# A hybrid pooling and state-space layer on one core: the scan's groups of four heads taken in pairs, nine small transposes in one place, and the first gate sum next to a pair

## The chip, the core and the metric

One core of a Trainium2 chip runs the whole layer in one launch. The metric is device time in microseconds (us), the median of three runs. Five engines work side by side, each through its own queue in order: PE (TensorE, the matmuls; PEld is its weight loading), DVE (VectorE), ACT (ScalarE), POOL (GpSimd) and SP (SyncE, which issues most transfers).

## What is computed

256 prompt positions and 32 sample positions are held as 288 columns (features lie on partitions). All matrices and data are fp32. The part that the change touches is the mixer of the layer, cut to what matters:

```python
proj = rmsnorm(x) @ w_in             # columns u | z | xBC | dt
xbc  = silu(causal_dwconv(xBC))      # xs (2048), B (2 groups x 128), C (2 x 128)
dt   = softplus(dt_raw + bias); a = dt * A        # 32 heads
acum = cumsum(a) ; lmat = exp(acum_l - acum_s) for s <= l
cb   = C_l . B_s                     # one per group of 16 heads
y    = (cb * lmat) @ (xs * dt) + exp(acum) * (C @ h_prev) + D * xs
y    = y * silu(z)
y    = y * rsqrt(mean(y*y) + eps) * norm_g        # per group of 16 heads
mix  = concat[pool, y] @ w_out
```

After it come the residual, the FFN (`w_up`, a short convolution, `silu(gate) * value`, `w_down`) and its norm, which the change leaves alone.

## The kernel before

**The large projections.** Every weight matrix is read from HBM in `raw` tiles of 1 MB. Each is split, 1024 columns at a time, into a high part and a low part: ACT copies `whi` (L129), then DVE subtracts to get `wlo` (L130). With an activation that was split in the same way, a product is three matmuls of 128x288 (`mm3`, L135 to L137: hi by hi, hi by lo, lo by hi). One pair of `whi` and `wlo`, called a weight tile below, feeds 24 such matmuls, and there are four buffers of each part, so the split can run at most four tiles ahead of PE. A call of `project` for 256 columns is a block of 96 matmuls, four weight tiles, into two accumulators `acc` (a PSUM pool of five, `acc_ps`).

**The order of the blocks.** First a block of 768 columns (B, C, the first 256 of xs), then seven blocks for the rest of xs, then eight for z, then four for u. In Python the scan's steps are written between the blocks; the scheduler of the language places every instruction on its engine's queue by its own timeline.

**The decays.** `g` (running sums of dt times A) and `dt` are 32 rows. Nine PE transposes (three each of `g`, `dt` and `dec`, L413 to L415) bring them to positions on partitions, three tiles `ptok` in PSUM; DVE copies them to `tok` and `tokd` (L416, L417). Then `pcb` (L430 to L432) makes the products of C and B, masked to `cbt`.

**A group of four heads (`ssd_four`, L442 to L485).** There are eight. SP fetches `gb` (the rows of g for four heads, broadcast to all partitions), `h0t` and `xw` (xs with positions on partitions, which went through DRAM as `xs_d` by way of `blocks_out`, one buffer `blocks`). ACT makes `ce`, then 12 activations write `m` from `gb` and `tok` (L464), then one Exp over all of `m` (L467). DVE scales `xw` (L459) and multiplies `m` by `cbt` (L469). PE then makes 16 products, which are 32 passes in the trace, into two PSUM tiles `py` (L476 to L482). DVE adds them into xs (L485). `gb`, `h0t`, `xw`, `ce` and `m` have two buffers each; `py` lies in the small PSUM pool `aux` with three buffers.

**When a group runs.** `XS_RATE` and `Z_RATE` say how many groups are written behind each block of xs and z. The gate multiplies the finished xs by silu(z) (`gate_in`, `gate_silu`, `gate_mul`), sums squares on POOL (`gsum`), and `gate_rstd` takes the mean by a matmul `psum_g` (L489) in `aux`, then Sqrt on ACT (L236) and a reciprocal on DVE (L237).

Of the kernel before, what the change touches and what calls it, by code (L numbers as in the profile page):

```python
# [8 lines left out]
F32 = mybir.dt.float32  # L9
F32R = mybir.dt.float32r  # L10
AF = mybir.ActivationFunctionType
ALU = mybir.AluOpType
# [4 lines left out]
P = 128  # L17
# [4 lines left out]
NT = NP_ + NS  # L22
# [3 lines left out]
HEADS = 32  # L26
# [3 lines left out]
NX = D_SSD // P  # L30
# [5 lines left out]
HALF = NF // 2  # L36
MW = 416
EVAC = 100
XS_RATE = (0, 0, 0, 1, 0, 1, 0, 1)
Z_RATE = (1, 0, 1, 0, 1, 1, 1, 0)  # L40


@with_exitstack
def body(
# [25 lines left out]
    act, dve, pool, pe, sp = nc.scalar, nc.vector, nc.gpsimd, nc.tensor, nc.sync  # L70
# [7 lines left out]
    acc_ps = ctx.enter_context(tc.tile_pool(name="acc_ps", bufs=5, space=PSUM))  # L78
# [3 lines left out]
    def aux(shape, name):  # L82
        return aux_ps.tile(shape, F32, tag="aux", name=name)
# [97 lines left out]
    mean = const.tile([P, P], F32, name="mean")  # L181
# [35 lines left out]
    start = ExitStack()  # L217
# [35 lines left out]
    for kb, n in chunks:  # L253
# [12 lines left out]
        for k in range(kb, kb + n):  # L266
# [19 lines left out]
            for m in range(6):  # L286
                c = slice(m * P, (m + 1) * P)
# [5 lines left out]
    p_ = aux([P, NT], "pdt")  # L293
# [23 lines left out]
    id32 = ident[:HEADS, :HEADS]  # L317
# [63 lines left out]
    dt = htile("dt", tag="gsum")  # L381
# [7 lines left out]
    g = mp.tile([HEADS, 2, MW], F32, tag="m", bufs=2, name="g")[:, 0, :]  # L389
# [11 lines left out]
    dec = htile("dec", tag="gsum")  # L401
# [4 lines left out]
    tok = mp.tile([P, 3, 2, HEADS], F32, name="tok")  # L406
    tokd = const.tile([P, 3, HEADS], F32, name="tokd")
    dec_s = mp.tile([HEADS, 4, NS], F32, name="dec_s")
    dve.tensor_copy(dec_s, dec[:, NP_:].unsqueeze(1).broadcast_to([HEADS, 4, NS]))
    dec_s = dec_s.rearrange("h r s -> h (r s)")  # L410
    for b, (go, o) in enumerate(((0, 0), (256, P), (288, NT - P))):
        p_ = aux([P, 3, HEADS], "ptok")
        pe.transpose(p_[:, 0, :], g[:, go : go + P], id32)  # L413
        pe.transpose(p_[:, 1, :], dt[:, o : o + P], id32)
        pe.transpose(p_[:, 2, :], dec_s if b == 2 else dec[:, o : o + P], id32)  # L415
        dve.tensor_copy(tok[:, b, :, :], p_[:, 0:2, :])  # L416
        dve.tensor_copy(tokd[:, b, :], p_[:, 2, :])  # L417

    bc = []
    for i in range(4):  # L420
        o = btile("bc")
# [17 lines left out]
    xs = []  # L439
    elast = const.tile([P, HEADS + 32], F32, name="elast")  # L440

    def ssd_four(q):  # L442

        c = slice(2 * P * q, 2 * P * q + 2 * P)
        gb = mp.tile([P, 4, MW], F32, tag="gb", bufs=2, name="gb")
        sp.dma_start(out=gb, in_=g_d[4 * q : 4 * q + 4, :].unsqueeze(0).broadcast_to([P, 4, MW]))
        h0t = mp.tile([P, 2 * P], F32, tag="h0t", bufs=2, name="h0t")
        sp.dma_start(out=h0t, in_=state_ssd[:, c])
        xw = mp.tile([P, 3, 2 * P], F32, tag="xw", bufs=2, name="xw")
        sp.dma_start(out=xw[:, 0:2, :], in_=xs_d[:NP_, c].rearrange("(b p) c -> p b c", p=P))  # L450
        sp.dma_start(out=xw[:, 2, :], in_=xs_d[NT - P :, c])
        ce = mp.tile([P, 4, NS], F32, tag="ce", bufs=2, name="ce")
        act.activation(ce, gb[:, :, 384:], AF.Exp)
        act.activation(elast[:, 4 * q : 4 * q + 4], gb[:, :, MW - 1], AF.Exp)
        cs = bc[2 + q // 4][:, NP_:]
        dve.tensor_tensor(ce, ce, cs.unsqueeze(1).broadcast_to([P, 4, NS]), op=ALU.mult)
        w = tok[:, :, 1, 4 * q : 4 * q + 4].unsqueeze(3).broadcast_to([P, 3, 4, 64])
        x4 = xw.rearrange("p b (r q) -> p b r q", r=4)
        dve.tensor_tensor(x4, x4, w, op=ALU.mult)  # L459
        m = mp.tile([P, 4, MW], F32, tag="m", bufs=2, name="m")  # L460
        for j in range(4):
            h = 4 * q + j
            for b, (lo_, hi_) in enumerate(((0, 256), (256, 384), (384, MW))):
                act.activation(  # L464
                    m[:, j, lo_:hi_], gb[:, j, lo_:hi_], AF.Relu, bias=tok[:, b, 0, h : h + 1], scale=-1.0
                )
        act.activation(m, m, AF.Exp, scale=-1.0)  # L467
        gi = q // 4
        dve.tensor_tensor(m, m, cbt[:, gi : gi + 1, :].broadcast_to([P, 4, MW]), op=ALU.mult)  # L469
        ys = [aux([P, NT], "py") for _ in range(2)]  # L470
        for k in range(4):
            for j in range(4):
                c = slice(64 * j, 64 * j + 64)
                y = ys[j // 2][64 * (j % 2) : 64 * (j % 2) + 64, :]
                if k == 0:
                    pe.matmul(y[:, 0:256], xw[:, 0, c], m[:, j, 0:256], start=True, stop=False)  # L476
                elif k == 1:
                    pe.matmul(y[:, 128:256], xw[:, 1, c], m[:, j, 256:384], start=False, stop=True)  # L478
                elif k == 2:
                    pe.matmul(y[:, 256:], xw[:, 2, c], m[:, j, 384:], start=True, stop=False)  # L480
                else:
                    pe.matmul(y[:, 256:], h0t[:, c], ce[:, j, :], start=False, stop=True)  # L482
# [4 lines left out]
    def gate_rstd(t):  # L487
        p_ = aux([P, NT], "psum_g")
        pe.matmul(p_, mean, gsum[t], start=True, stop=True)  # L489
# [13 lines left out]
    gsum = [mp.tile([P, NT], F32, tag="gsum", bufs=2, name="gsum") for _ in range(2)]  # L503
# [31 lines left out]
    fours = list(range(NX // 2))  # L535
    gates = list(range(NX))
    done = [-1]
    rg = []

    def run_fours(n):  # L540
        for _ in range(n):
            if fours and 2 * fours[0] + 1 < len(xs):
                q = fours.pop(0)
                ssd_four(q)
                done[0] = 2 * q + 1

    def run_gates():
        while gates and gates[0] in zs and gates[0] <= done[0]:
# [7 lines left out]
    for i in range(NX // 2):  # L556
        ps = project(win, [(O_Z + 256 * i, 256)], xn, K16)
        for j in range(2):
            gate_in(2 * i + j, ps[j])
        if i == 0:  # L560
            xs_conv(NX // 2 - 1)
        run_fours(Z_RATE[i])
        for j in range(2):
            gate_silu(2 * i + j)
        run_gates()
        if i == 4:
            assert gates[0] >= 8
            rg.append(gate_rstd(0))
        if i > 4:
            for t in range(3 * i - 15, min(8, 3 * i - 12)):  # L570
                dve.tensor_tensor(xs[t], xs[t], rg[0], op=ALU.mult)
    run_fours(NX)
    run_gates()
    assert not gates and not fours

# [76 lines left out]
    for t in range(NX):  # L652
# [4 lines left out]
        _, low = split_from(a, xs[t], g_ssd[:, t : t + 1])  # L657
# [150 lines left out]
    for grp in ((0, 1), (2,), (3,), (4,), (5,), (6,), (7,)):  # L808
# [5 lines left out]
        if grp[0] == 2:  # L814
            j = grp[0] // 2 - 1
# [51 lines left out]
    for k in range(KD):  # L867
# [15 lines left out]
        else:  # L883
            q = out_temp()
# [357 lines left out]
```

## Time and profile before

| | |
|---|---|
| time, median of 3 runs | 1320.09 us (1319.91 to 1320.91) |
| the profiled execution's own time | 1319.88 us |
| its span (first to last instruction) | 1317.90 us |
| granted TensorE clock | 0.999 |
| DVE busy | 894.7 us (68%) |
| ACT busy | 670.9 us (51%) |
| POOL busy | 232.6 us (18%) |
| HBM | 188 GB/s over the span |

An engine's share says how busy it was over all stages. Rows of the timeline give the start in us, the length in us, engine, line, operation, output and inputs, and how many like instructions follow each other (x8); in brackets stands idle time ahead of it and what ended it. A matmul's length is its latency; the next one starts long before it ends, so what a matmul costs is read from start to start. Rows of groups give the sum of busy time, the mean length of one in ns, and the idle time ahead of them.

### The profile page before, as it was taken

To read this page: it belongs to the slowest core of one execution; us is meant where nothing else is said; L and a number is where in the kernel's file an instruction comes from. 1 tells how busy PE (TensorE), PEld (TensorE's weight loads), DVE (VectorE), ACT (ScalarE), POOL (GpSimd) and SP (SyncE) were. 2 spreads that over 40 slices of the span, in tenths; PEclk is the share of its full clock that TensorE was granted. 3 is DMA by queue.
4 is the path that set the end of the run, shared out by engine and by line. 5 is a ranking of instruction groups with operands and counts; after the bars stand their busy time and mean duration, and the time that the engine had idled before them with its cause. 6 is when DMAs were issued, how large, how long until landed. Compare 5 with 4: busy or idle time off the path is not lost.

```text
span 1317.9 us, 25200 instructions
## 1 busy us (share of the span) xinstructions
PE 1310.9 (99%) x10067; PEld 1298.6 (99%) x10067; DVE 894.7 (68%) x1486; ACT 670.9 (51%) x1010; POOL 232.6 (18%) x368
## 2 busy tenths in 40 slices
PE   9999999999999999999999999999999999999998
PEld 9999999999999999999999999999999999999997
DVE  7999997779654599967766743346666666664544
ACT  7558876446543466644444433334444444444443
POOL 7321221221430200211211200001111111101110
PEclk9999999999999999999999999999999999999999
DMA  8668874465665556666544445455544554466663
GB/s 327 200 206 280 277 233 144 150 227 205 203 211 192 180 169 221 185 185 194 172 165 160 156 172 173 155 177 180 173 161 164 177 172 160 163 235 187 204 178 110
DMA packets 104068, 249.81 MB, mean 190 GB/s; under 512 B 64064, under 2 KB 69504, under 8 KB 81680
## 3 DMA queue, kind: packets, MB, share of 16 engines
q1 hardware_dynamic: 101584, 242.72, 56.0%
q0 software_dynamic: 1936, 5.31, 1.4%
q8 instruction: 78, 1.28, 0.4%
q14 instruction: 38, 0.31, 0.1%
q10 hardware_dynamic: 432, 0.19, 0.1%
HBM read 236.23 MB, written 11.95 MB: 188 GB/s over the span
## 4 chain that ended last, share of the span: by engine, by line
PE 99%; DMA 1%; ACT 0%; SPq 0%; issue 0%; DVE 0%
PE acc L135 31%; PE acc L137 31%; PE acc L136 31%; PE py L476 1%; PE acc_x L135 1%; PE acc_x L137 1%; PE acc_x L136 1%; DMA raw<-in_w_first 1%; PE pst L773 0%; PE run_a L1114 0%; PE low L1112 0%; PE run_b L1127 0%; PE py L478 0%; PE pdt L297 0%; PE py L482 0%; PE py L480 0%
## 5 line engine op out<-in xcount | busy, mean ns | idle before, releaser
L130 DVE TENSOR_TENSOR wlo<-raw,whi 128x1024 fp32r<-128x1024 f32 (+1 forms) x386 | 463.0, 1201 | 313.2 <-ACT whi L129 310.7
L129 ACT ACTIVATE whi<-raw 128x1024 fp32r<-128x1024 f32 (+1 forms) x386 | 400.2, 1038 | 463.3 <-PE acc L136 370.5
L135 PE MATMUL acc<-hn,whi 128*128 128x288 f32 x1360 | 393.3, 294 | 0.0
L136 PE MATMUL acc<-hn,whi 128*128 128x288 f32 x1360 | 392.7, 293 | 0.0
L137 PE MATMUL acc<-hn,wlo 128*128 128x288 f32 x1360 | 391.9, 293 | 0.0
L135 PEld LDWEIGHTS acc<-hn,whi 128*128 128x128 f32 x1360 | 253.3, 188 | 0.4 <-ACT hn L873 0.4
L136 PEld LDWEIGHTS acc<-hn,whi 128*128 128x128 f32 x1360 | 253.3, 188 | 0.1
L137 PEld LDWEIGHTS acc<-hn,wlo 128*128 128x128 f32 x1360 | 253.3, 188 | 0.0
L135 PE MATMUL acc<-xn,whi 128*128 128x288 f32 x688 | 202.5, 296 | 0.7 <-ACT whi L276 0.7
L136 PE MATMUL acc<-xn,whi 128*128 128x288 f32 x688 | 200.3, 293 | 0.0
L137 PE MATMUL acc<-xn,wlo 128*128 128x288 f32 x688 | 195.0, 295 | 0.0
L135 PE MATMUL acc<-fa,whi 128*128 128x288 f32 x660 | 194.0, 294 | 0.0
L136 PE MATMUL acc<-fa,whi 128*128 128x288 f32 x660 | 193.4, 293 | 0.0
L137 PE MATMUL acc<-fa,wlo 128*128 128x288 f32 x660 | 193.1, 293 | 0.0
L135 PEld LDWEIGHTS acc<-xn,whi 128*128 128x128 f32 x688 | 129.3, 188 | 2.6 <-ACT whi L276 1.2
L136 PEld LDWEIGHTS acc<-xn,whi 128*128 128x128 f32 x688 | 129.2, 188 | 0.4
L137 PEld LDWEIGHTS acc<-xn,wlo 128*128 128x128 f32 x688 | 126.5, 188 | 0.0
L135 PEld LDWEIGHTS acc<-fa,whi 128*128 128x128 f32 x660 | 124.1, 188 | 0.0
L137 PEld LDWEIGHTS acc<-fa,wlo 128*128 128x128 f32 x660 | 123.9, 188 | 0.0
L136 PEld LDWEIGHTS acc<-fa,whi 128*128 128x128 f32 x660 | 123.9, 188 | 0.0
L925 POOL COPY fc_stage<-ebuf 128x4 f32<-128x4 f32 x88 | 27.7, 315 | 513.7 <-DVE ebuf L924 513.7
L921 POOL COPY ebuf<-pf 128x2 f32<-128x2 f32 x88 | 75.5, 858 | 129.5 <-DVE fc L931 83.0
(312 smaller groups left out, 1742.2 us busy)
## 6 DMA issues: line engine op xcount, KB each, us to landing
raw<-in_w_up SPq DMA_DIRECT2D x80, 1024.0 KB, 4.8
raw<-in_w_in SPq DMA_DIRECT2D x38, 1024.0 KB, 5.0
raw<-in_w_down SPq DMA_DIRECT2D x32, 1024.0 KB, 4.8
raw<-in_w_out SPq DMA_DIRECT2D x23, 1024.0 KB, 4.8
raw<-in_w_down SPq DMA_DIRECT2D x16, 768.0 KB, 4.3
raw<-in_w_up SPq DMA_DIRECT2D x8, 896.0 KB, 4.5
gb<-g_d SPq DMA_DIRECT2D x8, 832.0 KB, 6.2
raw<-in_w_first SPq DMA_DIRECT2D x7, 768.0 KB, 10.0
```

The costliest lines, as they stand in the source:

```text
L129: act.activation(hi, raw[:, k : k + n, :], AF.Copy)
L130: dve.tensor_tensor(lo, raw[:, k : k + n, :], hi.bitcast(F32), op=ALU.subtract)
L135: pe.matmul(out, wh, a[:, 0, :], start=start, stop=False)
L136: pe.matmul(out, wh, a[:, 1, :], start=False, stop=False)
L137: pe.matmul(out, wl, a[:, 0, :], start=False, stop=stop)
L476: pe.matmul(y[:, 0:256], xw[:, 0, c], m[:, j, 0:256], start=True, stop=False)
L921: pool.tensor_copy(e[:, 258:260], pf[:, 4:6, i])
L925: pool.tensor_copy(fc_stage[:, :, :, i], e[:, 256:324].rearrange("p (s c) -> p s c", c=34)[:, :, 0:2])
```

## The change

The eight groups of four are taken two by two: behind the last xs block, and behind the third, fifth and seventh z block (counted from one). `ssd_four` is cut in two. `four_in` is everything up to the product of `m` and `cbt`; `four_out` holds the PE products and the addition into xs. `run_fours` calls `four_in` for both groups and then `four_out` for both: the first matmul may not be issued before the second group's `m` is done, and the 32 products (64 passes) are kept in the order written. Their four PSUM tiles are three of `aux` and one of the accumulators' pool.

The nine transposes go into one PSUM tile in one go, in a fixed order, and two DVE copies take all of it. The matmul of the first gate sum is written ahead of the third pair, and pinned there.

```diff
-XS_RATE = (0, 0, 0, 1, 0, 1, 0, 1)
-Z_RATE = (1, 0, 1, 0, 1, 1, 1, 0)
+XS_RATE = (0, 0, 0, 0, 0, 0, 0, 2)
+Z_RATE = (0, 0, 2, 0, 2, 0, 2, 0)
...
-    for b, (go, o) in enumerate(((0, 0), (256, P), (288, NT - P))):
-        p_ = aux([P, 3, HEADS], "ptok")
-        pe.transpose(p_[:, 0, :], g[:, go : go + P], id32)
-        pe.transpose(p_[:, 1, :], dt[:, o : o + P], id32)
-        pe.transpose(p_[:, 2, :], dec_s if b == 2 else dec[:, o : o + P], id32)
-        dve.tensor_copy(tok[:, b, :, :], p_[:, 0:2, :])
-        dve.tensor_copy(tokd[:, b, :], p_[:, 2, :])
+    def tok_out():
+        p_ = aux([P, 3, 3, HEADS], "ptok")
+        jobs = [(2, 2, dec_s)] + [(b, 2, dec[:, P * b : P * b + P]) for b in range(2)]
+        for b, (go, o) in enumerate(((0, 0), (256, P), (288, NT - P))):
+            jobs += [(b, 0, g[:, go : go + P]), (b, 1, dt[:, o : o + P])]
+        for n, (b, i, src) in enumerate(jobs):
+            ins = pe.transpose(p_[:, b, i, :], src, id32)
+            if n:
+                tc.keep_in_program_order(ins)
+        dve.tensor_copy(tok, p_[:, :, 0:2, :])
+        dve.tensor_copy(tokd, p_[:, :, 2, :])
...
-    def ssd_four(q):
+    def four_in(q):
...
-        dve.tensor_tensor(m, m, cbt[:, gi : gi + 1, :].broadcast_to([P, 4, MW]), op=ALU.mult)
-        ys = [aux([P, NT], "py") for _ in range(2)]
+        got = dve.tensor_tensor(m, m, cbt[:, gi : gi + 1, :].broadcast_to([P, 4, MW]), op=ALU.mult)
+        return xw, h0t, ce, m, got
+
+    def four_out(q, ys, xw, h0t, ce, m, _, after=None):
+
+        ops = []
...
+        for y, w_, v_, go, end in ops:
+            with ExitStack() as order:
+                if after is not None:
+                    order.enter_context(tc.issue_after(after.ins))
+                ins = pe.matmul(y, w_, v_, start=go, stop=end)
+            tc.keep_in_program_order(ins)
+            after = None
...
     def run_fours(n):
-        for _ in range(n):
-            if fours and 2 * fours[0] + 1 < len(xs):
-                q = fours.pop(0)
-                ssd_four(q)
-                done[0] = 2 * q + 1
+        qs = [fours.pop(0) for _ in range(n) if fours]
+        if not qs:
+            return
+        assert 2 * qs[-1] + 1 < len(xs)
+        got = [four_in(q) for q in qs]
+        ys = [aux([P, NT], "py") for _ in range(3)] + [acc_ps.tile([P, NT], F32, tag="acc", name="py_a")]
+        for i, q in enumerate(qs):
+            four_out(q, ys[2 * i : 2 * i + 2], *got[i], after=None if i else got[-1][-1])
+        done[0] = 2 * qs[-1] + 1
...
+        if i == 4:
+            assert gates[0] >= 8
+            rg.append(gate_rstd(0, True))
         run_fours(Z_RATE[i])
...
-        if i == 4:
-            assert gates[0] >= 8
-            rg.append(gate_rstd(0))
...
-    run_fours(NX)
```

**How the instructions move.** On PE, near the 680th projection matmul, the transposes stood before in several places between the projection's matmuls (`ptok` is the transposes' PSUM tile, `acc` the projection's accumulator):

```order
L137 MATMUL acc<-xn,wlo 128x288
L413 MATMUL ptok<-ident,g 128x32
L414 MATMUL ptok<-ident,dt 128x32
L135 MATMUL acc<-xn,whi 128x288
L413 MATMUL ptok<-ident,g 128x32
L414 MATMUL ptok<-ident,dt 128x32
L413 MATMUL ptok<-ident,g 128x32
L414 MATMUL ptok<-ident,dt 128x32
L136 MATMUL acc<-xn,whi 128x288
```

The transposes of `dec` came 33 and 48 projection matmuls later, and `pcb` another 18 after that. Now, behind the 727th projection matmul:

```order
L135 MATMUL acc<-xn,whi 128x288
L417 MATMUL ptok<-ident,dec_s 128x32
L417 MATMUL ptok<-ident,dec 128x32 x2
L417 MATMUL ptok<-ident,g 128x32
L417 MATMUL ptok<-ident,dt 128x32
L417 MATMUL ptok<-ident,g 128x32
L417 MATMUL ptok<-ident,dt 128x32
L417 MATMUL ptok<-ident,g 128x32
L417 MATMUL ptok<-ident,dt 128x32
L436 MATMUL pcb<-bc 128x256
```

All nine stand together, directly ahead of `pcb`. The products of the groups of four stood in nine places (one group's in two halves), after 833, 838, 868, 960, 1056, 1248, 1440, 1536 and 1632 projection matmuls; now they stand in four, after 960, 1248, 1440 and 1632.

On PE after the 1440th projection matmul, with the numbers of the tiles and the semaphores that a row waits for (`psum_g` is the gate's sum; `py_2886` to `py_2888` lie in `aux`, `py_a` among the accumulators), pieces of the new order:

```order
L506 MATMUL psum_g_2827<-gsum_826,mean_84 128x288 [waits PE_49,Pool_49]
L497 MATMUL py_2886<-m_2844,xw_2836 64x256 [waits DMAHW2_49,PE_49]
L497 MATMUL py_2886<-m_2844,xw_2836 64x256
L497 MATMUL py_2887<-m_2844,xw_2836 64x256 [waits PE_49]
L497 MATMUL py_2886<-ce_2839,h0t_2834 64x32 [waits DMAHW3_49]
L497 MATMUL py_2887<-ce_2839,h0t_2834 64x32 x2
L497 MATMUL py_2888<-m_2871,xw_2863 64x256 [waits DMAHW3_49,Activation_49]
```

The sum stood behind the products of its place before and stands ahead of them now; `py_2888`, the third tile that the pair takes of `aux`, waits for ACT, which reads `psum_g` out of the buffer that both use. On ACT that read (L236) stands directly behind a table load, and that behind the fourth `whi` that follows this place.

On DVE behind the first pair, while the second is made ready (`m_2473` and `m_2500` are its two `m`; `z` are the two accumulators of the first z block):

```order
L475 TENSOR_TENSOR m_2473<-m_2473,cbt_795 128x1664
L130 TENSOR_TENSOR wlo_2208<-raw_2205,whi_2207 128x1024
L347 SCALAR_TENSOR_TENSOR conv_1909<-ebuf4_673,pah_123,conv_1909 128x291
L171 STREAM_TRANSPOSE blocks_1777<-xs_1766 128x288
L130 TENSOR_TENSOR wlo_2212<-raw_2205,whi_2211 128x1024
L529 TENSOR_TENSOR z_2153<-acc_2035,rstd_126 128x288
L347 SCALAR_TENSOR_TENSOR conv_1926<-ebuf5_674,pah_123,conv_1926 128x291
L347 SCALAR_TENSOR_TENSOR conv_1909<-ebuf4_673,pah_123,conv_1909 128x291
L529 TENSOR_TENSOR z_2155<-acc_2036,rstd_126 128x288
L475 TENSOR_TENSOR m_2500<-m_2500,cbt_795 128x1664
L347 SCALAR_TENSOR_TENSOR conv_1926<-ebuf5_674,pah_123,conv_1926 128x291
L130 TENSOR_TENSOR wlo_2266<-raw_2263,whi_2265 128x1024
```

Both products of `m` now stand within three `wlo` of each other. On ACT, ahead of `whi_2207` and behind the `whi` before it, stand 24 activations of `m`, two `ce`, two tanh and the first Exp in a row. Before, this stretch held one group's.

More of the change, by code (lines that the diff above doesn't have):

```diff
@@ L410, in body @@
     dec_s = dec_s.rearrange("h r s -> h (r s)")
-    for b, (go, o) in enumerate(((0, 0), (256, P), (288, NT - P))):
-        p_ = aux([P, 3, HEADS], "ptok")
-        pe.transpose(p_[:, 0, :], g[:, go : go + P], id32)
-        pe.transpose(p_[:, 1, :], dt[:, o : o + P], id32)
-        pe.transpose(p_[:, 2, :], dec_s if b == 2 else dec[:, o : o + P], id32)
-        dve.tensor_copy(tok[:, b, :, :], p_[:, 0:2, :])
-        dve.tensor_copy(tokd[:, b, :], p_[:, 2, :])
+    def tok_out():
[9 more added lines that the diff above has]
+        dve.tensor_copy(tokd, p_[:, :, 2, :])
+    tok_out()
     bc = []
@@ L475, in ssd_four @@
                 if k == 0:
-                    pe.matmul(y[:, 0:256], xw[:, 0, c], m[:, j, 0:256], start=True, stop=False)
+                    ops.append((y[:, 0:256], xw[:, 0, c], m[:, j, 0:256], True, False))
                 elif k == 1:
-                    pe.matmul(y[:, 128:256], xw[:, 1, c], m[:, j, 256:384], start=False, stop=True)
+                    ops.append((y[:, 128:256], xw[:, 1, c], m[:, j, 256:384], False, True))
                 elif k == 2:
-                    pe.matmul(y[:, 256:], xw[:, 2, c], m[:, j, 384:], start=True, stop=False)
+                    ops.append((y[:, 256:], xw[:, 2, c], m[:, j, 384:], True, False))
                 else:
-                    pe.matmul(y[:, 256:], h0t[:, c], ce[:, j, :], start=False, stop=True)
+                    ops.append((y[:, 256:], h0t[:, c], ce[:, j, :], False, True))
+        for y, w_, v_, go, end in ops:
[5 more added lines that the diff above has]
+            after = None
         for i in range(2):
@@ L485, in ssd_four, with gate_rstd @@
             dve.scalar_tensor_tensor(xs[t], xs[t], dcol[:, t : t + 1], ys[i], op0=ALU.mult, op1=ALU.add)
-    def gate_rstd(t):
+    def gate_rstd(t, pin=False):
         p_ = aux([P, NT], "psum_g")
-        pe.matmul(p_, mean, gsum[t], start=True, stop=True)
+        ins = pe.matmul(p_, mean, gsum[t], start=True, stop=True)
+        if pin:
+            tc.keep_in_program_order(ins)
         o = const.tile([P, NT], F32, tag="spread", bufs=3, name="rg")
```

## The prediction

> **What bounds the kernel now.** I read the page first, its busy shares and its chain of waits, then the timeline of PE around the scan, then ACT and DVE in the same stretch.
>
> ```profile
> PE 1310.9 (99%) x10067; PEld 1298.6 (99%) x10067; DVE 894.7 (68%) x1486; ACT 670.9 (51%) x1010; POOL 232.6 (18%) x368
> PE 99%; DMA 1%; ACT 0%; SPq 0%; issue 0%; DVE 0%
> ```
>
> PE is never idle for long, and the chain that ended last is PE for 99%. So the time is the sum of what PE's queue costs from start to start: any PE time removed is gained in full, and any new wait of PE is paid in full. Nothing later gives it back. The timeline of PE at one group of four:
>
> ```profile
> 158.93 0.29 PE L136 MATMUL acc<-xn,whi 128*128 128x288 f32 x1
> 159.06 0.29 PE L137 MATMUL acc<-xn,wlo 128*128 128x288 f32 x1
> 159.29 1.08 PE L476 MATMUL py<-m,xw 128*64 128x256 f32 x8
> ...
> 161.18 0.40 PE L135 MATMUL acc<-xn,whi 128*128 128x288 f32 x1
> 161.42 0.29 PE L136 MATMUL acc<-xn,whi 128*128 128x288 f32 x1
> 126.18 0.65 PE L476 MATMUL py<-m,xw 128*64 128x256 f32 x4
> ...
> 127.19 0.40 PE L136 MATMUL acc<-xn,whi 128*128 128x288 f32 x1
> ```
>
> Projection matmuls follow each other every 0.13. Going over to the small products costs 0.23 (159.06 to 159.29), 0.10 more; coming back costs 0.24 (161.18 to 161.42), 0.11 more. Inside, 32 passes take 1.89 (159.29 to 161.18) and 16 passes take 1.01 (126.18 to 127.19), so 16 more cost 0.88 and 0.12 is fixed. One visit costs 0.10 + 0.11 + 0.12 = 0.33 beside its passes.
>
> **What the change removes.** Nine visits of products become four, with the same passes: 5 x 0.33 = 1.65. The nine transposes:
>
> ```profile
> 98.49 0.29 PE L137 MATMUL acc<-xn,wlo 128*128 128x288 f32 x1
> 98.72 0.24 PE L413 MATMUL ptok<-ident,g 32*128 32x32 f32 x1
> ...
> 109.26 0.59 PE L430 MATMUL pcb<-bc 128*128 128x256 f32 x2
> ```
>
> From 98.49 to 109.26 are 10.77, in which 68 projection matmuls were started (67 between the four visits, and the one at 98.49); 68 x 0.131 = 8.91, so the transposes cost 1.86. In one run directly ahead of `pcb` they cost one way in (0.10) and nine passes at some 0.06 to 0.07 (98.72 to 98.80 is 0.08), 0.7 in all. Gain 1.15. The gate's sum shared a visit before and shares one now: 0. Together PE's queue gets 2.8 shorter. That is a count of instructions at measured prices, and I hold it for nearly certain.
>
> **What it adds: a wait for a PSUM buffer.** The sum is now ahead of the pair, and the pair's third `aux` tile needs its buffer back, after ACT's Sqrt.
>
> ```profile
> 213.48 0.45 ACT L515 ACTIVATE tanh_z<-z 128x288 f32<-128x288 f32 x1 [1.72 <-DVE z L510]
> 213.86 1.06 ACT L129 ACTIVATE whi<-raw 128x1024 fp32r<-128x1024 f32 x1
> ...
> 215.63 1.90 ACT L464 ACTIVATE m<-gb,tok 128x256 f32<-128x256 f32 x6
> 217.44 0.29 ACT L453 ACTIVATE ce<-gb 128x128 f32<-128x128 f32 x1
> 217.64 1.91 ACT L464 ACTIVATE m<-gb,tok 128x256 f32<-128x256 f32 x6
> 219.56 1.28 ACT L236 ACT_TABLE_LOAD   x1
> 220.85 0.50 ACT L236 ACTIVATE rg<-psum_g,eps_t 128x288 f32<-128x288 f32 x1
> 213.82 1.08 PE L476 MATMUL py<-m,xw 128*64 128x256 f32 x8
> ...
> 215.71 0.75 PE L489 MATMUL psum_g<-gsum,mean 128*128 128x288 f32 x2
> 216.09 0.51 PE L135 MATMUL acc<-xn,whi 128*128 128x288 f32 x1
> ```
>
> Call T the start of PE's visit, here 213.82. A `whi` starts at T + 0.04, because PE's last matmul frees its buffer. In the new order the table load comes next, then the Sqrt: T + 0.04 + 1.06 + 1.28 + 0.50 = T + 2.9. PE asks for the tile after the sum (216.09 - 215.71 = 0.38) and 32 passes (1.77): T + 2.15. It waits 0.75; I take 0.8. The bounds are 0 (a `whi` that comes earlier) and 1.8 (one more `whi` ahead of it). Behind the waiting matmul stand the pair's second half and the whole next block.
>
> The row speaks against a rule here. The Trainium skill (ScalarE: Activation LUTs, What ACT_TABLE_LOAD costs) counts a load of 1283 ns and a drain of some 1380 ns for every switch; by it the wait would be about 2.1 and the forecast 1.4 higher. In the trace the Sqrt starts 1.29 after the load, with no drain, so the sum goes by the row.
>
> **What it adds: lumps on ACT and DVE.** PE needs a new weight tile every 24 x 0.131 = 3.15, and the split is at most four tiles ahead. The groups on ACT and DVE around the scan:
>
> ```profile
> L129 ACT ACTIVATE whi<-raw 128x1024 fp32r<-128x1024 f32 x49 | 51.5, 1055 | 26.9 <-PE acc L136 25.2 <-issue 1.7
> L467 ACT ACTIVATE m<-m 128x1664 f32<-128x1664 f32 x8 | 12.7, 1584 | 0.0
> L130 DVE TENSOR_TENSOR wlo<-raw,whi 128x1024 fp32r<-128x1024 f32 x50 | 61.5, 1233 | 14.0 <-ACT whi L129 13.9
> L469 DVE TENSOR_TENSOR m<-m,cbt 128x1664 f32<-128x1664 f32 x8 | 15.7, 1959 | 0.6 <-ACT m L467 0.6
> L459 DVE TENSOR_TENSOR xw<-xw,tok 128x768 f32<-128x768 f32 x8 | 7.6, 953 | 3.6 <-DMA xw<-xs_d 3.5
> L171 DVE STREAM_TRANSPOSE blocks<-xs 128x288 f32<-128x288 f32 x13 | 6.1, 472 | 3.9 <-DMA xs_d<-blocks 3.9
> xs_d<-blocks SPq DMA_DIRECT2D x51, 36.0 KB, 4.1
> ```
>
> Making one group ready holds ACT for 3.9 (12 activations and `ce`, 215.63 to 219.56) and an Exp of 1.5, DVE for 1.9 and 0.9. How much cover that leaves, where one group is made at a time:
>
> ```profile
> 230.50 2.36 DVE L130 TENSOR_TENSOR wlo<-raw,whi 128x1024 fp32r<-128x1024 f32 x2
> 234.15 0.29 PE L135 MATMUL acc<-xn,whi 128*128 128x288 f32 x1
> 116.64 1.22 DVE L130 TENSOR_TENSOR wlo<-raw,whi 128x1024 fp32r<-128x1024 f32 x1
> 121.11 0.29 PE L135 MATMUL acc<-xn,whi 128*128 128x288 f32 x1
> 196.01 1.83 DVE L130 TENSOR_TENSOR wlo<-raw,whi 128x1024 fp32r<-128x1024 f32 x1
> 197.76 2.50 DVE L469 TENSOR_TENSOR m<-m,cbt 128x1664 f32<-128x1664 f32 x1
> 201.14 0.29 PE L135 MATMUL acc<-xn,whi 128*128 128x288 f32 x1
> ```
>
> The first `wlo` at 230.50 ends at about 231.7 and PE uses it at 234.15: 2.4 of cover. The one at 116.64 leaves 3.25, the one at 196.01 leaves 3.3. A pair puts a second 3.9 + 1.5 = 5.4 on ACT and 2.8 on DVE into nearly the same stretch, and its second half keeps PE only 1.77 longer. 2.4 to 3.3 of cover does not hold 3.6 more. Pair by pair, with T the start of the visit that frees the buffers:
>
> Second pair (T after 960 projection matmuls). ACT starts on it at T + 1.6, when the first `m` is free; 7.85 for 24 activations and two `ce`, 0.7 for two tanh, 1.5 for the Exp bring the next `whi` to T + 11.65. PE needs that tile at T + 3.65 + 0.2 + 4 x 3.15 = T + 16.4. DVE multiplies `m` (to T + 13.6) and has `wlo` at T + 14.8: in time. The next `wlo` stands behind the second `blocks`, whose one buffer is free when four transfers have landed (four issues of some 0.45, then 4.1): T + 18, so `wlo` at T + 19.2 against T + 19.55. Then DVE has two evacuations, three convolution steps and the other `m` (about 3.8) ahead of the third `wlo`: T + 24.1 against T + 22.7, of which 0.26 is covered because `wlo` is the third matmul's. That is 1.1 at median landings; the waits of DVE on `xw` and `blocks` in the rows above show that some are late. 0 to 4, I take 2.0.
>
> First pair. `tok` is now one copy that needs all nine transposes, and it stands behind a `wlo` and a convolution step, some 2.2 later than the copies in the profile; the ACT work behind it is the same. The cover of 3.25 becomes about 0 to 1 two tiles on, and a `blocks` wait follows. 0 to 3, I take 1.5.
>
> Third pair. Three squares, two tanh, 24 activations, two `ce` and an Exp (11.1) stand between two `whi`: the next starts at T + 12.2. With the lengthened rows at 196.01 and 197.76 (1.83 and 2.50; POOL was adding) DVE ends its `wlo` at T + 16.3 against T + 16.4. 0 to 2.5, I take 1.2. Fourth pair: Sqrt, second table load (1.28), 7.85, Exp: `whi` at T + 13.5, `wlo` about T + 16.5 against T + 17.5. 0 to 1, I take 0.3.
>
> **The sum.** -2.8 + 0.8 + 2.0 + 1.5 + 1.2 + 0.3 = +3.0. The profiled execution took 1319.88 (span 1317.90 and 1.98 around it), so 1322.9; the median of the runs is 0.2 above that execution, so 1323.1 for the median. Where a lump on ACT ends, nothing else becomes late: after the last pair the order of all engines is nearly as before, and the second gate sum keeps its place.
>
> **The rivals.**
>
> 1. The cover holds. Late tiles are made up because ACT is idle 26.9 in this stretch, mostly waiting for PE to free `whi` buffers. For it: the average load is low, and no group more is computed. Against it: the idle time lies between the lumps. With the buffer wait of 0.8 alone: 1319.9 - 2.8 + 0.8 + 0.2 = 1318.1; with that hidden too, 1317.3, which is the other side.
>
> 2. The stalls about equal the gain: some 2 to 4 in all, only the second pair and the buffer wait. For it: the lower half of each bound. 1320 to 1321.
>
> 3. The transfers decide. In the second pair `xw` of both groups is fetched in one go behind the visit, among 1 MB weight tiles, and DVE's queue holds `xw` ahead of `wlo`. If those land late by twice the 4.1 median, three pairs lose up to 4, 3 and 2.5: with the buffer wait some 10, 1319.9 - 2.8 + 10.3 + 0.2 = 1327.6. For it: the 3.5 and 3.9 of idle time on `xw` and `blocks` that DVE already has. Against it: these are seen with fewer transfers at once as well.
>
> That the visits don't get fewer is excluded by the order on PE.
>
> **Chances.** Forecast 0.48, the cover holds 0.20, an even score 0.22, late transfers 0.10. 0.2% of the time (2.6) is about what a measurement of this kernel can tell from no change. Faster by more than that needs practically no stall at all: 0.13, part of the first rival. Slower by more: the third rival and most of the forecast, 0.51. Within: 0.36. The range goes from the first rival without the buffer wait, 1317.2, to the third, 1328.
>
> **What would show it.** Right on the gain: four visits of 3.65 in PE's timeline in place of nine, `ptok` and `pcb` side by side. Right on the buffer wait: the row of `py` in the third visit with 0.5 to 1 of idle time put down to `rg` L236. Right on the lumps: idle time of PE ahead of L135 and L137 on `acc`, released by `whi` or `wlo`, in the blocks after the visits and ahead of the first, between 0.3 and 2 each; the sum of these against 2.8 settles the sign. Wrong: a scan without such rows, or PE's fixed cost of a visit not falling with the number of visits.

## The result, and the profile after

| | before | changed |
|---|---|---|
| median of 20 runs each | 1320.37 us (1319.59 to 1323.24) | 1323.58 us (1320.73 to 1328.09) |
| ratio, with its 95% interval | | 1.0020 (1.0014 to 1.0026) |
| profiled execution | 1319.88 us, span 1317.9 | 1321.71 us, span 1320.0 |

The change is slower by 2.6 (0.0020 of 1320.4) by the ratio, 3.2 between the medians. Two things stand out: its profiled execution lies 1.9 under its own median, and its runs spread over 7.4, twice as wide as before. First the page of the changed kernel, the busy times and the chain that ended last:

```profile
PE 1309.4 (99%) x10067; PEld 1297.7 (98%) x10067; DVE 893.8 (68%) x1482; ACT 671.9 (51%) x1010; POOL 228.2 (17%) x368
PE 97%; DMA 1%; ACT 1%; DVE 1%; issue 0%; SPq 0%; DVEq 0%; ACTq 0%
```

Then its waits of PE between 60 and 330 (in all, how often, the longest). In the kernel before, this view lists no wait at all.

```profile
PE acc L137 <- DVE wlo L130: 2.0, 2, 1.6
PE psum_g L506 <- POOL gsum L520: 0.4, 1, 0.4
PE py L497 <- ACT rg L236: 0.4, 1, 0.4
```

PE is busy 1.5 less than before (1310.9), and yet the span is 2.1 longer. ACT and DVE now own a share of the chain. Idle time is counted from the modelled end of a matmul and so falls short; what a wait costs is read from start to start. The timeline of PE at the transposes and around the third visit:

```profile
106.29 0.24 PE L417 MATMUL ptok<-ident,dec_s 32*128 32x32 f32 x1
...
106.96 0.70 PE L436 MATMUL pcb<-bc 128*128 128x256 f32 x2
182.27 0.65 PE L497 MATMUL py<-m,xw 128*64 128x256 f32 x4
...
185.93 0.40 PE L135 MATMUL acc<-xn,whi 128*128 128x288 f32 x1
...
212.98 0.29 PE L137 MATMUL acc<-xn,wlo 128*128 128x288 f32 x1
213.66 0.75 PE L506 MATMUL psum_g<-gsum,mean 128*128 128x288 f32 x2 [0.38 <-POOL gsum L520]
...
216.66 0.65 PE L497 MATMUL py<-m,xw 128*64 128x256 f32 x4 [0.36 <-ACT rg L236]
...
218.55 0.40 PE L135 MATMUL acc<-xn,whi 128*128 128x288 f32 x1
```

The nine transposes take 0.67 (106.29 to 106.96), and 0.10 on the way in, in place of 1.86 in several places. The second visit takes 3.66 (182.27 to 185.93). Between it and the third lie 192 matmuls, which need 192 x 0.131 = 25.15; they took 27.73 (185.93 to 213.66), an excess of 2.58. I call this the excess of a stretch; 0.13 to 0.25 of it is the fixed cost at its two ends, the rest is waiting. The third visit takes 4.89.

This account by stretches, worked out in the same way from the starts of the visits, is the yardstick for all runs with pairs. "To first pair" is counted from behind `pcb`.

| kernel | its profiled run | to first pair | to second | to third | third visit | to fourth |
|---|---|---|---|---|---|---|
| changed | 1321.71 | 0.58 | 1.06 | 2.58 | 4.89 | 0.28 |
| changed, second profile | 1321.40 | 0.36 | 1.70 | 1.87 | 4.89 | 0.30 |
| changed, third profile | 1324.91 | 0.36 | 0.57 | 5.41 | 4.91 | 1.01 |
| pairs only | 1324.08 | 0.27 | 3.93 | 0.98 | 4.89 | 0.28 |
| sum with its own buffer | 1324.60 | 3.25 | 1.03 | 2.28 | 4.34 | 0.33 |
| second xw later | 1322.74 | 1.49 | 1.25 | 1.77 | 4.90 | 0.28 |
| two blocks buffers | 1321.58 | 0.25 | 2.20 | 0.37 | 4.89 | 0.33 |
| second input later | 1318.20 | 0.23 | 0.26 | 0.16 | 4.94 | 0.25 |
| second input later, own buffer | 1318.00 | 0.23 | 0.26 | 0.15 | 4.23 | 0.23 |
| second input later, own buffer, two blocks buffers | 1318.47 | 0.24 | 1.21 | 0.14 | 4.23 | 0.23 |
| second input later, own buffer, old transposes | 1320.54 | 0.23 | 0.37 | 1.20 | 4.23 | 0.23 |

The first, second and fourth visit take 3.65 or 3.66 in every row. Line numbers shift by a few where an edit adds lines.

### The profile page after: what moved, and what is told of

Same layout as the page of the kernel before. It is cut to its first block, busy times and chain, and to the rows that moved or that the text cites. A ratio compares the mean times of both kernels' runs of the same rounds, so it can differ in the third digit from the quotient of the medians.

```text
span 1320.0 us, 25192 instructions
## 1 busy us (share of the span) xinstructions
PE 1309.4 (99%) x10067; PEld 1297.7 (98%) x10067; DVE 893.8 (68%) x1482; ACT 671.9 (51%) x1010; POOL 228.2 (17%) x368
## 4 chain that ended last, share of the span: by engine, by line
PE 97%; DMA 1%; ACT 1%; DVE 1%; issue 0%; SPq 0%; DVEq 0%; ACTq 0%
PE acc L137 30%; PE acc L135 30%; PE acc L136 30%; PE py L497 1%; PE acc_x L135 1%; PE acc_x L137 1%; PE acc_x L136 1%; DMA raw<-in_w_first 1%; DMA out<-sc_stage 1%; PE pst L795 0%; PE run_a L1136 0%; PE low L1134 0%; DVE wlo L130 0%; PE run_b L1149 0%; PE py_a L497 0%
## 5 line engine op out<-in xcount | busy, mean ns | idle before, releaser
L953 DVE SCALAR_TENSOR_TENSOR fc<-ebuf,pf,fc 128x290 f32<-128x290 f32 x176 | 90.0, 516 | 2.6
```

What stands on the lines that cost most here:

```text
L953: dve.scalar_tensor_tensor(c, e[:, r_ : r_ + 290], pf[:, r_, i : i + 1], c, op0=ALU.mult, op1=ALU.add)
```

## The experiments

Theory A: the inputs of two groups, made in one go, fill ACT and DVE, and the weight tiles behind them are late. Theory B: DVE stands still for late transfers (`blocks`, `xw`) with weight tiles queued behind.

### One part alone

**Only the nine transposes in one visit**, everything else as before the change (the scheduler then joins the two halves of one group, so there are eight visits of products in place of nine):

```diff
-        p_ = aux([P, 3, HEADS], "ptok")
+        p_ = aux([P, 3, 3, HEADS], "ptok")
...
-        dve.tensor_copy(tok[:, b, :, :], p_[:, 0:2, :])
+        dve.tensor_copy(tok, p_[:, :, 0:2, :])
```

> Only the nine transposes in one visit; the groups of four run singly, as before the change. Theory A (visits of PE gain, only the pairs stall): the profile of the change puts the one visit at 0.96 gained, and the order on PE saves one visit of products more (0.33), so 1319.0 to 1319.4. Rival B (the transposes in one go make tok late, and that alone makes weight tiles late in the 150 matmuls behind it): stalls of L137 ahead of the first groups, 1320.4 to 1321.5.

Measured 1323.37, ratio 1.0019 (1.0010 to 1.0028). Theory A's 1319.0 to 1319.4 is missed by 4. The profiled run (1324.50) has an excess of 5.2 in one stretch, the 192 matmuls ahead of the visit that the gate's sum shares. One row of the waits of DVE (110 to 250):

```profile
DVE blocks L171 <- DMA xs_d<-blocks: 7.5, 5, 2.8
```

DVE and PE in its timeline:

```profile
185.07 0.48 DVE L171 STREAM_TRANSPOSE blocks<-xs 128x288 f32<-128x288 f32 x1 [2.40 <-DMA xs_d<-blocks]
...
202.25 1.21 DVE L130 TENSOR_TENSOR wlo<-raw,whi 128x1024 fp32r<-128x1024 f32 x1
...
203.51 0.40 PE L137 MATMUL acc<-xn,wlo 128*128 128x288 f32 x1 [2.43 <-DVE wlo L130]
```

The loss isn't where rival B placed it, in the 150 matmuls behind the late `tok`, but some 70 us further on: DVE stood still for `blocks` five times, 7.5 in all, and its backlog reaches PE at the first tile behind a group's inputs. Of the 5.2, 3.2 is waiting (2.6 of it at 203.51, 0.6 at the `whi` ahead of it); another 1.5 is lost behind the wait, where from 204.9 to 208.0 the matmuls start 0.24 apart in place of 0.13, at a granted clock of 0.50. More on this below, at the third profile of the change. The same row of the kernel before is

```profile
DVE blocks L171 <- DMA xs_d<-blocks: 1.3, 1, 1.3
```

I read this as a sign that even one group at a time is sensitive to where the waits for transfers stand on DVE's queue.

**Only the pairs**, the transposes as before:

```diff
-    tok_out()
+    for b, (go, o) in enumerate(((0, 0), (256, P), (288, NT - P))):
+        p_ = aux([P, 3, HEADS], "ptok")
```

> The pairs and the gate's sum ahead of the third, with the transposes in several places as before the change. Theory A (the loss is the pairs'): 1.65 gained on visits, and the stalls of the change's profile but for the first pair's 0.36 (which A puts down to the late tok): 0.8 + 2.3 + 0.9, so 1320.4 + 2.4 = 1322.8, with the same spread of several us between runs. Rival B (the late tok is the cause, the pairs alone are harmless): 1318.7 to 1319.5.

Measured 1325.06 in five runs, ratio 1.0037 (1.0024 to 1.0050), 2.3 above theory A's 1322.8. The late `tok` isn't the cause of the loss: without it the first pair has no stall (0.27), the other two still have. The second pair lost 3.7 in this profile and 0.8 in the first of the change.

### The buffer of the gate's sum

```diff
-        ys = [aux([P, NT], "py") for _ in range(3)] + [acc_ps.tile([P, NT], F32, tag="acc", name="py_a")]
+        n_aux = 2 if len(fours) == 2 else 3
+        ys = [aux([P, NT], "py") for _ in range(n_aux)]
+        ys += [acc_ps.tile([P, NT], F32, tag="acc", name="py_a") for _ in range(4 - n_aux)]
```

> The change, but the third pair takes two of its four PSUM tiles from the accumulators' pool, so that none shares a buffer with the gate's sum; the order on every engine stays. Theory A (the wait for the Sqrt costs what it shows): the third visit falls from 4.89 to 4.0 or 4.1 and the time by 0.8, 1322.7 to 1322.9. Rival B (the wait only hides another: the next block's tiles or the evacuation of z are late then): the visit gets shorter, and the same 0.8 shows up in the 96 matmuls behind it, 1323.5.

Measured 1322.13, ratio 1.0013 (1.0004 to 1.0022). The visit fell from 4.89 to 4.34 here and to 4.23 in the run further down, and no more excess stands behind it (0.33 against 0.28): the wait for the Sqrt costs 0.55 here, 0.71 between the two kernels with the second input held back (4.94 against 4.23), and hides nothing. The interval overlaps that of the change, so only the profile settles the size. The profiled run lost 3.0 in another place, ahead of the first pair, where the order on every engine is that of the change.

### Theory A against theory B

**ACT's work for the second group held back**, behind the high part of a later weight tile (third to fifth from the last one written):

```diff
-                act.activation(hi, raw[:, k : k + n, :], AF.Copy)
+                whis.append(act.activation(hi, raw[:, k : k + n, :], AF.Copy))
...
-        got = [four_in(q) for q in qs]
+        got = [four_in(qs[0])]
+        with tc.issue_after(whis[(-4, -5, -3, -3)[qs[0] // 2]].ins):
+            got.append(four_in(qs[1]))
```

> The change, but ACT's work for the second group of each pair is queued behind the weight tile that comes some tiles later, so that the two groups' inputs are not made in one go; the visits of PE are the same four. Theory A (two groups' inputs in one go on ACT and DVE make the tiles late): the stalls of 0.4, 0.8 and most of 2.3 go, the wait for the Sqrt (0.9) stays, 1320.0 to 1320.8 and a narrower spread between runs. Rival B (late transfers through the one buffer of blocks make the tiles late, whatever ACT does): the stalls stay, 1322.5 to 1324, and runs spread as wide as those of the change (1320.7 to 1328.1).

Measured 1318.23, ratio 0.9986 (0.9977 to 0.9995), below even the range of theory A; 10 of 11 runs lie within 1.7 of each other, one at 1322.15. All stalls at weight tiles are gone (0.23, 0.26, 0.16). The only wait of PE that is left is that of `py` for the Sqrt, 0.5.

PE, ACT and DVE in its timeline ahead of the third pair:

```profile
181.14 0.65 PE L498 MATMUL py<-m,xw 128*64 128x256 f32 x4
...
187.40 1.58 ACT L474 ACTIVATE m<-m 128x1664 f32<-128x1664 f32 x1
188.89 1.04 ACT L130 ACTIVATE whi<-raw 128x1024 fp32r<-128x1024 f32 x1
...
191.50 0.96 DVE L466 TENSOR_TENSOR xw<-xw,tok 128x768 f32<-128x768 f32 x1 [5.04 <-DMA xw<-xs_d]
192.38 1.89 DVE L476 TENSOR_TENSOR m<-m,cbt 128x1664 f32<-128x1664 f32 x1
194.53 0.96 DVE L466 TENSOR_TENSOR xw<-xw,tok 128x768 f32<-128x768 f32 x1 [0.26 <-DMA xw<-xs_d]
195.40 2.36 DVE L131 TENSOR_TENSOR wlo<-raw,whi 128x1024 fp32r<-128x1024 f32 x2
```

The same place in the change (SPq is SP's queue issuing transfers):

```profile
181.56 0.48 DVE L171 STREAM_TRANSPOSE blocks<-xs 128x288 f32<-128x288 f32 x1 [2.32 <-DMA xs_d<-blocks]
...
186.43 0.45 ACT L534 ACTIVATE tanh_z<-z 128x288 f32<-128x288 f32 x1 [0.96 <-DVE z L529]
...
189.23 1.83 SPq L174 DMA_DIRECT2D xs_d<-blocks  x4
...
191.72 0.43 SPq L456 DMA_DIRECT2D xw<-xs_d  x1
194.88 1.58 ACT L473 ACTIVATE m<-m 128x1664 f32<-128x1664 f32 x1
...
196.57 1.05 ACT L129 ACTIVATE whi<-raw 128x1024 fp32r<-128x1024 f32 x1
196.38 0.96 DVE L465 TENSOR_TENSOR xw<-xw,tok 128x768 f32<-128x768 f32 x1 [2.32 <-DMA xw<-xs_d]
197.26 1.89 DVE L475 TENSOR_TENSOR m<-m,cbt 128x1664 f32<-128x1664 f32 x1
199.06 3.58 DVE L130 TENSOR_TENSOR wlo<-raw,whi 128x1024 fp32r<-128x1024 f32 x2
200.94 0.40 PE L137 MATMUL acc<-xn,wlo 128*128 128x288 f32 x1 [1.60 <-DVE wlo L130]
```

Both kernels wait for `xw`; the one that loses nothing waits longer in one piece (5.04 for the first group's, against 2.32 for the second's). The difference is what stands behind the wait. With the second input held back, `whi` starts 7.75 after the visit (181.14 to 188.89), and the product of the first `m` fits in between the two transfers, so two `wlo` follow at once. In the change `whi` starts 14.3 after the visit (182.27 to 196.57), since 23 of the two groups' 24 activations ran ahead of the first Exp; the product of `m` comes behind the second `xw`, and `wlo` behind that. The wait of 2.32 explains at most 0.80 of the 1.9 lost here: the Exp ends at 196.46 (194.88 + 1.58), so the product, which started at 197.26, could not have started earlier than that. The rest is ACT's own lateness and a slower `wlo` (3.58 for two, against 2.36).

The edit binds ACT's queue alone, but the other queues move with it: the second `xw` of this pair is issued 3.7 behind the visit's start (at 184.84), and in the change 9.45 behind it (182.27 to 191.72), after four transfers of `blocks`. So this run shows that the order with ACT's work held back cures the loss, and not that ACT's lump was the whole of it.

**Only DVE's wait for the second `xw` held back**, ACT's work in one go as in the change:

```diff
-        dve.tensor_tensor(x4, x4, w, op=ALU.mult)
+        with ExitStack() as order:
+            if behind is not None:
+                order.enter_context(tc.issue_after(behind.ins))
+            dve.tensor_tensor(x4, x4, w, op=ALU.mult)
...
-        got = [four_in(q) for q in qs]
+        got = [four_in(qs[0]), four_in(qs[1], wlos[(-4, -5, -3, -3)[qs[0] // 2]])]
```

> The change, but only DVE's scaling of the second group's xw is queued behind a later weight tile (four to six of them), so that its wait for the transfer no longer stands ahead of the first tiles; ACT's 24 activations for the two groups stay in one go. Theory A (ACT's lump of two groups is what makes the tiles late; holding it back alone took 1318.2): the stalls stay within 1 us of the change's, 1322.5 to 1324. Theory B (the wait for xw on DVE is): the second and third pair lose their stalls (0.8 and 1.9), 1320 to 1321.

Measured 1322.41, ratio 1.0012 (1.0004 to 1.0021), 1.2 under the change and just under the range of theory A. Two of its waits of PE, and two of DVE's (110 to 250):

```profile
PE psum_g L510 <- POOL gsum L524: 1.4, 1, 1.4
PE acc L138 <- DVE wlo L131: 1.2, 2, 0.6
DVE blocks L172 <- DMA xs_d<-blocks: 8.4, 6, 2.9
DVE xw L469 <- DMA xw<-xs_d: 2.9, 1, 2.9
```

In the change these two rows are

```profile
DVE xw L465 <- DMA xw<-xs_d: 6.5, 2, 4.2
DVE blocks L171 <- DMA xs_d<-blocks: 5.4, 3, 2.8
```

The waits moved: those for `xw` fell, those for `blocks` rose, and ahead of the third pair PE no longer waits for a weight tile but for the gate's sum, whose last two squares ACT starts at 210.44, after 2.81 of waiting for DVE's product of xs and z. So taking one wait for `xw` off DVE's queue is not enough. That the lump on ACT is what must go is the likelier reading, and not shown apart from the orders that move with it.

**Two buffers for `blocks`**, the change otherwise (the scheduler moves some rows by it):

```diff
-        s = pool_.tile([P, NT], F32, tag="blocks", bufs=1, name="blocks")
+        s = pool_.tile([P, NT], F32, tag="blocks", bufs=2 if pool_ is mp else 1, name="blocks")
```

> The change with two buffers for blocks in place of one, so that DVE's transpose of one xs tile needn't wait for the transfers of the one before; both groups of a pair are still made ready in one go. The scheduler moves some rows by it. Theory B (DVE stands still for late transfers, 5.4 on blocks and 6.5 on xw in the change's profile against 1.3 and 3.5 before it, with weight tiles queued behind): the waits on blocks fall below 1.5 and the stalls of the first and second pair (0.4 and 0.8, more in slow runs) go, 1320 to 1321.5. Theory A (the two groups' work itself fills DVE and ACT): the stalls stay, 1323 to 1324.

Measured 1321.69, ratio 1.0012 (1.0001 to 1.0022), runs from 1319.09 to 1327.55. DVE's waits for `blocks` are gone, those for `xw` are 7.4. The stall ahead of the third pair went with them (2.58 to 0.37), though ACT still makes both groups ready in one go. Two things come earlier there: the second `xw`, which in the change is fetched behind four transfers of `blocks` on SP's queue (189.23, 191.72 above), starts on DVE 12.4 behind the visit's start in place of 14.1, and the next `whi` starts 12.1 behind it (183.18 to 195.24) in place of 14.3. So at this pair the lump fits its cover when the wait of 2.32 for `blocks` ahead of it is gone. The second pair still loses 2.0 and the spread stays. So theory B names part of the loss, and this buffer does not cure it.

**The transposes alone, with two buffers for `blocks`:**

> Only the nine transposes in one visit, groups singly, and two buffers for blocks. With one buffer this took 1323.4, with DVE waiting 7.5 for blocks and a stall of 5.0 ahead of the third group from the end in its profile. Theory B (waits of DVE for late transfers ahead of weight tiles): that stall goes, 1318.7 to 1319.6. Theory A (one visit of transposes makes tok late and the groups bunch up behind it): still 1322 or more.

Measured 1320.32, ratio 0.9998 (0.9989 to 1.0007). The 3 that the transposes alone had lost are back, as theory B has it, but the 0.7 to 1.6 of gain expected isn't there; its profile (1319.64) has one stall of 0.8 behind the first groups, which there takes most of the gain of 1.1.

### The change again

> The change once more, for one profile more of runs that spread from 1320.7 to 1328.1. Theory: PE's visits and the wait for the Sqrt cost the same to 0.1 (2.45, 3.65, 3.65, 4.9 and 3.65), and what differs from the first profile (1321.7) lies in the matmuls ahead of the first three pairs, with weight tiles as releasers. Rival: the difference lies outside the scan (input, FFN, output).

> As the run before it, a third profile of the change. Theory: the visits as in the others to 0.1, and the difference in time is that of the stalls ahead of the first three pairs. Rival: the difference lies outside the scan.

1321.40 and 1324.91, one run each. The visits agree with the first profile to 0.02 (second and third row of the table). Of the 3.5 between the two, 3.1 lie in the stretches of the table (sums 9.12 and 12.26), and behind the second gate sum all three profiles take 1047.0 to 1047.1, so the difference is not outside the scan. The third profile's timeline ahead of the third pair:

```profile
197.07 0.96 DVE L465 TENSOR_TENSOR xw<-xw,tok 128x768 f32<-128x768 f32 x1 [3.46 <-DMA xw<-xs_d]
...
202.24 0.40 PE L137 MATMUL acc<-xn,wlo 128*128 128x288 f32 x1 [3.42 <-DVE wlo L130]
...
203.56 0.45 PE L136 MATMUL acc<-xn,whi 128*128 128x288 f32 x1
...
206.20 0.45 PE L137 MATMUL acc<-xn,wlo 128*128 128x288 f32 x1
206.44 0.37 PE L135 MATMUL acc<-xn,whi 128*128 128x288 f32 x1
```

The chain is the one shown for the change, with `xw` some 1.2 later behind the visit's start (a wait of 3.46). PE loses 3.6 by it, and then something that no account of waits shows: from 203.56 to 206.44 the matmuls take 0.45 and start 0.24 apart, in place of 0.29 and 0.13. The granted clock from 203.4 to 206.6 is 0.50; in the 8 us ahead of the stall and in the 3.4 behind this stretch it is 1.00. That costs another 1.5, nearly half of the 3.1 between the two profiles. Among the scans profiled here only this one and that of the transposes alone (a stall of 2.7 start to start, with one of 0.7 three us before it) have such a stretch; a single stall of 2.8 with the pairs only was not followed by one. So a long stall of PE can cost more than its own length. Where the limit lies is not shown.

### Versions without the stalls

The second input held back and the third pair's own buffers:

> The second input of each pair held back, as in the run of 1318.2, and the third pair's tiles not shared with the gate's sum. Theory A: the third visit (4.94 there) falls to 4.0, nothing becomes late behind it, 1317.2 to 1317.5. Rival: what was hidden by the wait of 0.9 (weight tiles or z's evacuation) takes its place, 1318.0 to 1318.4.

Measured 1317.88, ratio 0.9980 (0.9971 to 0.9989), all 11 runs within 1.7, between the ranges of the theory and of the rival. The view of PE's waits is empty again, and the third visit takes 4.23:

```profile
209.91 0.29 PE L138 MATMUL acc<-xn,wlo 128*128 128x288 f32 x1
210.04 0.65 PE L507 MATMUL psum_g<-gsum,mean 128*128 128x288 f32 x2
...
214.27 0.40 PE L136 MATMUL acc<-xn,whi 128*128 128x288 f32 x1
```

This beats both kernels: 0.2% under the kernel before.

With the two `blocks` buffers on top:

> All three: the second input held back, no buffer shared with the gate's sum, two buffers for blocks. The visits saved are worth 2.6, and with no stall left PE's queue would end at 1320.4 - 2.6 = 1317.8, less what little stall there was before the change. Theory A and B agree on 1317.0 to 1317.8, with all runs within 1 us; if some other wait of DVE or ACT is left, single runs lie 1 to 4 higher.

1318.25, ratio 0.9982 (0.9973 to 0.9991): no further gain and above the range expected, with a stall of 1.0 to the second pair in its profile. The same 1317.9 kernel with the transposes in several places:

> The second input held back and the third pair's own buffers, as in the run of 1317.9, with the transposes in their several places as before the change. Without stalls this prices the one visit of the transposes: by the count of 1.15 (0.96 between the profiles of before and of the change) the time is 1318.8 to 1319.1. Rival (where the late tok uses up cover, the one visit gains nothing net): 1317.6 to 1318.2.

1318.90, ratio 0.9990 (0.9981 to 0.9999): 1.0 more, as the count of the visits said, though the two intervals overlap a little. (Its profiled run, 1320.54, also lost 1.0 at one weight tile ahead of the third pair, so the held-back order isn't free of late tiles in every run.)

## Why the prediction came out, point by point

The forecast was 1323.1 for the median and the median is 1323.58; the direction and the kind of the waits that it named were right. Most of the sizes were not, two costs were missing from it (the wait for POOL's sum, and the half clock behind a long stall), and part of the agreement is luck.

- **Visits: right.** Four visits of 3.65 and nine transposes in one. The transposes gained 1.86 - 0.67 - 0.10 = 1.09 against 1.15, and 1.0 between the last kernel and the one without that part. Where no tile is late, nearly the whole gain shows: 1320.34 before against 1317.88 is 2.5 of the 2.8.
- **"It waits 0.75; I take 0.8": right, a little large.** The Sqrt ended at 216.61, T + 2.95, where T + 2.9 was said. The wait costs 0.55 to 0.71 by the visit's length with and without it. In this trace too the load starts right behind the `whi` ahead of it, and the Sqrt 1.30 after the load's start. By an estimate from the Trainium skill (ScalarE: Activation LUTs, What ACT_TABLE_LOAD costs), which counts a drain as well, the wait would have been some 2.1. This trace doesn't agree:

```profile
213.75 1.04 ACT L129 ACTIVATE whi<-raw 128x1024 fp32r<-128x1024 f32 x1
214.81 1.28 ACT L236 ACT_TABLE_LOAD   x1
216.11 0.50 ACT L236 ACTIVATE rg<-psum_g,eps_t 128x288 f32<-128x288 f32 x1
```

- **Second pair, 2.0: the tiles' times were right, the price wasn't.** The rows of the change's timeline (T is 139.83):

```profile
151.41 1.05 ACT L129 ACTIVATE whi<-raw 128x1024 fp32r<-128x1024 f32 x1
152.53 0.96 DVE L465 TENSOR_TENSOR xw<-xw,tok 128x768 f32<-128x768 f32 x1 [4.18 <-DMA xw<-xs_d]
...
156.00 1.22 DVE L130 TENSOR_TENSOR wlo<-raw,whi 128x1024 fp32r<-128x1024 f32 x1
157.96 1.19 DVE L130 TENSOR_TENSOR wlo<-raw,whi 128x1024 fp32r<-128x1024 f32 x1
162.89 1.22 DVE L130 TENSOR_TENSOR wlo<-raw,whi 128x1024 fp32r<-128x1024 f32 x1
...
156.44 0.30 PE L135 MATMUL acc<-xn,whi 128*128 128x288 f32 x1
156.58 0.30 PE L136 MATMUL acc<-xn,whi 128*128 128x288 f32 x1
157.28 0.40 PE L137 MATMUL acc<-xn,wlo 128*128 128x288 f32 x1 [0.40 <-DVE wlo L130]
```

  `whi` was said for T + 11.65 = 151.48 and started at 151.41; the second and third `wlo` for 159.03 and 163.9 and ended at 159.15 and 164.11. The first `wlo`, said to be in time at T + 14.8 = 154.6, ended at 157.22, because DVE waited 4.18 for the second `xw`: that is the third rival's mechanism. The step that failed on the price is "of which 0.26 is covered because `wlo` is the third matmul's". The scheduler had itself put two more `whi` matmuls ahead of the first `wlo` matmul (156.44, 156.58) at this tile, and more at others, 0.26 of cover for each two. The stretch lost 0.84 in the first profile (1.06 less the 0.22 of its ends), 1.5 and 0.35 in the other two.
- **First pair, 1.5: too large**, for the same reason (at 123.66 eight matmuls with `whi` stand in a row): 0.36, 0.14 and 0.14 in three profiles. Its upper bound of 3 was met once, in the kernel with the sum's own buffer (3.0).
- **Third pair, 1.2: too small.** Weight tiles cost 1.9 in the first profile; in the third 3.6, and 1.5 more by the half clock behind the stall, so "any new wait of PE is paid in full" was too little there. "The next starts at T + 12.2" was 14.3: DVE waited 2.32 for `blocks` (181.56 above) ahead of the evacuation of z that ACT's tanh at 186.43 needs, and the activations of `m` stand behind that tanh; and the wait for `xw`, at most 0.80 of the 1.9, had been left out of this pair's sum. With two `blocks` buffers `whi` started at T + 12.1, as forecast, and no tile was late. The wait of `psum_g` for POOL's sum (it starts 0.68 behind the matmul ahead of it, 212.98 to 213.66, where 0.13 is free of waiting, 209.91 to 210.04 in the 1317.9 kernel) was not foreseen at all: the squares behind it were late on DVE and ACT as the tiles were.
- **Fourth pair, 0.3: 0.06 in two profiles, 0.8 in one.**
- **The sum.** For the profiled execution 1322.9 was said and 1321.71 measured; for the median 1323.1 and 1323.58. In the first profile the costs come to 0.6 + 0.84 + 0.36 + 1.9 + 0.55 (the wait for POOL's sum) + 0.06 = 4.3, where 5.8 was said; less the gain of 2.5 that is 1.8, and the profile lies 1.83 above the one before. The prediction took the median to lie 0.2 above the profile, as it did before the change. It lies 1.9 above: that the median came out within 0.5 is luck, made by stalls that differ from run to run. In the three profiles these hang on transfers that land later or earlier, a share of the third rival's mechanism. Its time of 1327.6 was reached by two of the 20 runs (1327.90 and 1328.09); they have no profile, so what made them long is not shown.
- **The first rival (the cover holds)** failed in the change and is what the order with the second input held back brings about.

Left open: why the transposes alone, with two `blocks` buffers, gain nothing, when the same visit is worth 1.0 in the kernel with the held-back input. Not tried: more buffers for `whi` and `wlo`, and the transfers moved with ACT's and DVE's order kept, which would part theory A from theory B at the third pair.

## What to carry to other kernels

Bundling small products saved a fixed 0.33 here for each visit that went, and it showed nearly in full only where what feeds them wasn't made in one go as well: hold the second input back on its engine's queue by a few tiles, so that the main stream's own tiles stand ahead of it. Count the cover in tiles of the main stream, and don't price a stall by the wait in its brackets: a wait of 5.04 cost nothing, and one of 2.32 explains at most 0.80 of the 1.9 lost behind it. Behind a long stall, read the starts of the matmuls too, since the clock may have fallen. Where runs of a changed kernel spread wider than before, one profile is a sample: take several and compare them stretch by stretch.

## What the runs showed that I had not expected

The part of the change with the surest gain, nine transposes in one visit, made the kernel 0.19% slower alone, by a stall some 95 us behind them. The runs with pairs and both inputs in one go spread over 2.8 to 8.5 us, those with the second input held back and own buffers over 1.7 to 2.3.

The clock may have a part in this spread. Two stalls were followed by some 3 us at a granted clock of 0.50, at a price of 1.5 each. Nine of the change's 20 runs were granted 0.997 or 0.998 in the mean, as the third profile was (0.997); they took 1322.97 or more, 1323.63 at their median. The eleven with 0.999 or 1.000 took 1322.32 at theirs. All but one of the 20 have no profile, so that such stretches made the difference is not shown.
